# A hybrid decoder layer: the transposed projections of both token groups made once, during the first group's attention

## The chip, the core and the metric

The kernel runs on one core of a Trainium2 chip. The metric is the device time of one execution in microseconds (us), the median of several runs. Engines are named as in the profile: PE is TensorE (PEld its weight loads), DVE VectorE, ACT ScalarE, POOL GpSimd, SP SyncE, which here only issues DMAs.

## The reference, cut to what matters

1024 tokens of width 1024 go through one decoder layer. After an RMS norm, one weight gives seven projections: queries, keys, values and a gate for four retention heads, and queries, keys and values for four heads of differential attention. Then come the output projection with a residual, and a layer of 16384 single-neuron experts, of which each token takes 16 in each of 8 heads.

```python
h = rmsnorm(x, norm_mix_g); proj = h @ w_in
rq, rk, rv, rg, dq, dk, dv = jnp.split(proj, IN_OFFSETS, axis=-1)
ret_out  = silu(rg) * rmsnorm(retention(rq, rk, rv))            # chunks of 128 tokens, a state S carried on
diff_out = rmsnorm(diff_attention(dq, dk, dv, lam), g) * 0.2     # causal: two softmaxes, p1 - lam * p2
x = x + concat([ret_out, diff_out]) @ w_out
# peer: q = xn @ wq; scores s against sub-keys; top 16 of each half; top 16 of their sums -> experts e, gates g
x = x + einsum('thk,thkd->td', g * gelu(einsum('thkd,td->thk', u[e], xn)), v[e])
out = rmsnorm(x, final_norm_g)
```

## The kernel before, in words

Tokens lie in eight tiles of 128. They form two groups: tiles 0 to 2 (384 tokens, "sparse") and tiles 3 to 7 (640 tokens, "dense"). Every matmul operand in float32 is split into a high and a low part (`hi`, `lo`), and a product is three matmuls: hi·hi, lo·hi and hi·lo. A weight block of 512 KB is loaded into `wraw`, ACT makes `whi` (L152), DVE makes `wlo` (L154); `chunk` does this.

`front` is the path of one group up to its expert routing and is a generator: at each `yield` the program may switch to another one. Its stages are: norm and transpose into `hx` (tiles `hh`, `hl`); `proj_n`, the projections that come out token-major (values `rv` and `dv`, later the gate `rg`; PSUM tile `psN`, 512 columns); for each head `ret_proj` and `att_proj`, the projections that come out transposed (queries and keys; PSUM tile `psT`, 384 columns in the first group, two halves of 320 in the second); for each head and tile `retention` and `attention`; then `rg`, the mix, the output projection and its norm; then routing, whose many top-k instructions are DVE's. The projections of head h+1 are woven among the tiles of head h. `attention` for a tile is a chain across engines: scores on PE (`psS`), row maximum on DVE (`Z`, L349), exponentials on ACT (`e`), their difference on DVE (L358 to L361, one L359 per tile), transposes (`psA`) and the product with the values (`pov`) on PE.

The first group's experts are gathered, 768 times 512 KB by POOL with indices (L860 and L867), each followed by one DVE instruction: L862 (`ug`, with a small read of its accumulator) or L869 (`sa`). Five buffers (`ug`) hold what is under way. The second group's experts are computed densely, all 128 blocks of 128 neurons, in the last stage, which is matmuls (`psH`, `kp`, `psV`); its partial sums in `psV` are added by DVE at L830.

What sets the order: the program is written as loops and weaves, and a scheduler fixes the order on each engine when the kernel is built. A gathered instruction of DVE is held by `gate` behind a marked DVE instruction; marks are taken at the yields of the second group's way up to its routing, 1.5 at each:

```python
run(gated(weave(until(gd, "routing"), sparse_routes(...), ROUTE, 1), PER[:2]))   # PER = (1.5, 1.5, 0.0)
```

So the number of yields there sets how many gathered instructions may stand early; those without a mark of their own wait for the last mark, which lies at the first block of the last stage. The whole order of the front part is these lines:

```python
run(until(gs, "normed")); front_consts(cst, cp, wp); run(until(gs, "mixed"))
run(weave(until(gs, "summed"), until(gd, "normed"), 15, 5))
run(weave(until(gd, "projected"), gs, 8, 19))
```

Of the kernel before, what the change touches and what calls it, by code (L numbers as in the profile page):

```python
# [13 lines left out]
F32 = mybir.dt.float32  # L14
# [84 lines left out]
def layer_kernel(ctx, tc, x, wt, wn, wo, wq, sk, ut, u, v, gmix, gffn, gfin, gsub, dlam, consts, alb, out):  # L99
# [6 lines left out]
    kd_d = tc.dram_tile([H, 2, P, T], F32, name="kd_d")  # L106
# [24 lines left out]

    def front(m, pp, cst, g0, nt, dense, late):
# [13 lines left out]

        def chunk(src, shape):

            raw = wp.tile(shape, F32, tag="raw", bufs=RAW, name="wraw")
            SY.dma_start(raw, src)  # L150
            hi = wp.tile(shape, F32R, tag="uh", bufs=2, name="whi")
            A.activation(hi, raw, AF.Copy)  # L152
            lo = wp.tile(shape, F32R, tag="ul", bufs=2, name="wlo")
            V.tensor_sub(lo, raw, hi.bitcast(F32))  # L154
            return hi, lo

        def mm(ps, a, b, start, stop):

            PE.matmul(ps, a[0], b[0], start=start, stop=False)
            PE.matmul(ps, a[0], b[1], start=False, stop=False)  # L160
            PE.matmul(ps, a[1], b[0], start=False, stop=stop)

        def at(ops, *ix):
            return [o[ix] for o in ops]
# [62 lines left out]
        hx = yield from split_t(normed, "h")  # L227

# [11 lines left out]
        yield from proj_n([wn[8 + c] for c in range(4)], hx, put_dv)  # L240
        yield "projected"
# [11 lines left out]
        def ret_proj(h):  # L253
            qT = wp.tile([P, n], F32, tag="ga", bufs=2, name="qT")
            for a, b, ps in proj_t(wt[2 * h], hx):
                A.activation(qT[:, a:b], ps, AF.Copy)
            yield
            kT = ap.tile([P, n], F32, tag="kT", bufs=2, name="kT")
            for a, b, ps in proj_t(wt[2 * h + 1], hx):
                A.activation(kT[:, a:b], ps, AF.Copy, scale=P ** -0.5)  # L260
            ops[h] = [qT, kT]
            yield
# [30 lines left out]
        def att_proj(h):  # L293
            qa = [ap.tile([P, n], F32R, tag=f"q2{m}", bufs=2, name=f"qa{m}") for m in range(2)]
            qb = [ap.tile([P, n], F32R, tag=f"qb{m}", bufs=1, name=f"qb{m}") for m in range(2)]
            for a, b, ps in proj_t(wt[8 + 2 * h], hx):
                pt = ap.tile([P, b - a], F32, tag="pt", name="pt")
                A.activation(pt, ps, AF.Copy, scale=0.125)
                for m in range(2):
                    own, oth = slice(64 * m, 64 * m + 64), slice(64 - 64 * m, 128 - 64 * m)  # L300
                    A.activation(qa[m][own, a:b], pt[own], AF.Copy)
                    A.activation(qa[m][oth, a:b], pt[own], AF.Copy)
                    V.tensor_sub(qb[m][own, a:b], pt[own], qa[m][own, a:b].bitcast(F32))
                    V.tensor_sub(qb[m][oth, a:b], pt[own], qa[m][own, a:b].bitcast(F32))
            yield
            kk2 = ap.tile([P, 2, L], F32R, tag="kd", name="kk") if h % 2 else fp.tile([P, 2, L], F32R, tag="R", name="kk")
            kk = [kk2[:, m] for m in range(2)]
            if not first:
                for m, tl in enumerate(kk):
                    G.dma_start(tl[:, :lo0], kd_d[h, m][:, :lo0])  # L310
            for a, b, ps in proj_t(wt[8 + 2 * h + 1], hx):
                sl = slice(lo0 + a, lo0 + b)
                pt = ap.tile([P, b - a], F32, tag="pt", name="pt")
                A.activation(pt, ps, AF.Copy)
# [594 lines left out]
```

## Time and profile before

| | |
|---|---|
| median of 3 runs | 2905.25 us (2904.76 to 2907.47) |
| profiled execution, its own time | 2900.81 us |
| its span, first to last instruction | 2899.0 us |
| PE busy | 2712.1 us (94%) |
| DVE busy | 2363.5 us (82%) |
| ACT / POOL busy | 1063.9 us (37%) / 1047.4 us (36%) |
| granted PE clock, mean | 0.975 |

Busy time is the union of an engine's instructions; matmuls overlap in the pipeline, so a busy PE need not be working at its full rate. Read the table by stage rather than as a whole: the stages have different limits.

### The profile page before, as it was taken

The numbers are of one execution on the slowest core, as the hardware profiler recorded it, in microseconds if no ns is written. First come the engines' busy times: TensorE is split into PE (matmuls) and PEld (weight loads), VectorE is DVE, ScalarE is ACT, GpSimd is POOL, SyncE is SP. The second block draws the span as 40 slices with busy tenths as digits, with TensorE's granted clock in tenths as the row PEclk, the third lists the DMA queues.
The fourth block names the chain that finished last, engine by engine and source line by source line (L and its number), as shares of the span: only waits on it lengthen the run. The fifth ranks groups of instructions, "written<-read, shape, count | busy, mean of one in ns | idle before, by whom it ended". The sixth has DMA issues, their size and how long they took to land.

```text
span 2899.0 us, 43071 instructions
## 1 busy us (share of the span) xinstructions
PE 2712.1 (94%) x16043; PEld 2441.4 (84%) x16043; DVE 2363.5 (82%) x4547; ACT 1063.9 (37%) x1881; POOL 1047.4 (36%) x782
## 2 busy tenths in 40 slices
PE   7979988988889999998898998999999999999998
PEld 6868877876789999997787887899999999989987
DVE  3555899888589988985788887888889888888988
ACT  4653334544232369992222222222223222222222
POOL 0000004434310000003454443666565556655664
PEclk9989998999989999999999999999999999999999
DMA  5334236756742246668988898999999999999997
GB/s 167 105 126 146 95 113 234 242 195 236 246 150 82 87 153 236 250 257 299 313 303 285 307 326 289 347 321 344 337 333 351 325 345 341 336 343 326 341 339 259
DMA packets 292805, 741.34 MB, mean 256 GB/s; under 512 B 23401, under 2 KB 117609, under 8 KB 292594
## 3 DMA queue, kind: packets, MB, share of 16 engines
q0 software_dynamic: 111744, 404.28, 39.1%
q1 hardware_dynamic: 180850, 334.31, 33.4%
q8 instruction: 126, 2.06, 0.3%
q14 instruction: 85, 0.70, 0.1%
HBM read 670.14 MB, written 68.35 MB: 255 GB/s over the span
## 4 chain that ended last, share of the span: by engine, by line
PE 46%; DVE 14%; DMA 10%; issue 9%; POOL 3%; ACT 3%; SPq 0%; POOLq 0%; DVEq 0%; ACTq 0%
PE psH L721 6%; PE psH L722 6%; PE psH L720 6%; DMA gt<-g_d 4%; PE psV L794 4%; PE psV L795 3%; PE psV L796 3%; DMA ug<-in_u,idx 2%; PE kp L795 2%; PE kp L796 2%; PE kp L794 2%; PE psHs L720 2%; PE psHs L722 2%; DVE sa L869 2%; PE psHs L721 2%
## 5 line engine op out<-in xcount | busy, mean ns | idle before, releaser
L867 POOL DMA_INDIRECT vg<-in_v,idx x384 | 530.1, 1381 | 915.2 <-DVE ug L862 517.0
L860 POOL DMA_INDIRECT ug<-in_u,idx x384 | 511.9, 1333 | 502.7 <-DVE ug L862 335.4
L869 DVE SCALAR_TENSOR_TENSOR sa<-vg,shs,sa 128x1024 f32<-128x1024 f32 x384 | 491.9, 1281 | 40.5 <-DMA vg<-in_v,idx 36.9
L862 DVE SCALAR_TENSOR_TENSOR ug<-ug,sx 128x1024 f32<-128x1024 f32 x384 | 460.6, 1219 | 72.9 <-DMA ug<-in_u,idx 72.2
L720 PE MATMUL psH<-nh,uh 128*128 128x320 f32 x1424 | 439.6, 309 | 0.7 <-ACT uh L706 0.7
L721 PE MATMUL psH<-nl,uh 128*128 128x320 f32 x1424 | 439.7, 309 | 0.0
L722 PE MATMUL psH<-nh,ul 128*128 128x320 f32 x1424 | 438.6, 309 | 0.8 <-DVE ul L708 0.8
L794 PE MATMUL psV<-vh,wh 128*128 128x512 f32 x768 | 305.5, 399 | 29.3 <-DVE acc L830 27.5
L795 PE MATMUL psV<-vl,wh 128*128 128x512 f32 x768 | 304.4, 397 | 0.0
L796 PE MATMUL psV<-vh,wl 128*128 128x512 f32 x768 | 297.1, 397 | 0.0
L720 PEld LDWEIGHTS psH<-nh,uh 128*128 128x128 f32 x1424 | 267.4, 188 | 6.8 <-ACT uh L706 1.5
L721 PEld LDWEIGHTS psH<-nl,uh 128*128 128x128 f32 x1424 | 267.5, 188 | 5.1
L722 PEld LDWEIGHTS psH<-nh,ul 128*128 128x128 f32 x1424 | 267.2, 188 | 4.6 <-DVE ul L708 1.6
L723 ACT ACTIVATE ga<-psH 128x320 f32<-128x320 f32 x178 | 74.6, 426 | 407.5 <-PE psH L722 368.4
L706 ACT ACTIVATE uh<-uraw 128x1024 fp32r<-128x1024 f32 x128 | 135.6, 1059 | 207.1 <-PE psH L721 110.2
L720 PE MATMUL psHs<-nh,uh 128*128 128x320 f32 x624 | 197.0, 317 | 9.3 <-ACT ga L723 9.1
L154 DVE TENSOR_TENSOR wlo<-wraw,whi 128x1024 fp32r<-128x1024 f32 x104 | 126.7, 1219 | 93.0 <-ACT whi L152 90.9
L794 PEld LDWEIGHTS psV<-vh,wh 128*128 128x128 f32 x768 | 147.4, 192 | 61.9 <-DVE acc L830 30.5
L795 PE MATMUL kp<-vl,wh 128*128 128x512 f32 x512 | 198.3, 391 | 0.9 <-DVE vl L818 0.9
L152 ACT ACTIVATE whi<-wraw 128x1024 fp32r<-128x1024 f32 x104 | 110.0, 1058 | 241.6 <-PE psT L160 117.6
L794 PE MATMUL kp<-vh,wh 128*128 128x512 f32 x512 | 192.3, 391 | 5.3 <-ACT wh L810 5.3
L721 PE MATMUL psHs<-nl,uh 128*128 128x320 f32 x624 | 195.1, 313 | 0.0
(243 smaller groups left out, 6159.0 us busy)
## 6 DMA issues: line engine op xcount, KB each, us to landing
uraw<-in_ut SPq DMA_DIRECT2D x128, 512.0 KB, 6.3
vraw<-in_v SPq DMA_DIRECT2D x128, 512.0 KB, 6.8
g_d<-st SPq DMA_DIRECT2D x80, 512.0 KB, 4.9
gt<-g_d SPq DMA_DIRECT2D x32, 1280.0 KB, 18.0
wraw<-in_wt SPq DMA_DIRECT2D x32, 512.0 KB, 3.7
wraw<-in_wq SPq DMA_DIRECT2D x32, 512.0 KB, 3.7
hs_d<-ga SPq DMA_DIRECT2D x39, 320.0 KB, 2.5
gl<-hs_d SPq DMA_DIRECT2D x39, 320.0 KB, 6.8
```

Of the source, the lines that this page charges most:

```text
L154: V.tensor_sub(lo, raw, hi.bitcast(F32))
L706: A.activation(uh, raw, AF.Copy)
L720: PE.matmul(ps, uh[:, dc], xh[:, dc, sl], start=(dc == 0), stop=False)
L721: PE.matmul(ps, uh[:, dc], xl[:, dc, sl], start=False, stop=False)
L722: PE.matmul(ps, ul[:, dc], xh[:, dc, sl], start=False, stop=(dc == DC - 1))
L794: PE.matmul(ps, Wh[e][:, sl], Vh[e][:, so], start=start, stop=False)
L795: PE.matmul(ps, Wh[e][:, sl], Vl[e][:, so], start=False, stop=False)
L796: PE.matmul(ps, Wl[e][:, sl], Vh[e][:, so], start=False, stop=stop)
L860: G.indirect_dma_start(out=ug, out_offset=None, in_=u, in_offset=bass.IndirectOffsetOnAxis(ap=idxA[t][:, k:k + 1], axis=0))
L862: gate(V.scalar_tensor_tensor(ug, ug, 1.0, xt, op0=ALU.mult, op1=ALU.mult, accum_out=hs[:, k:k + 1]))
L867: G.indirect_dma_start(out=vg, out_offset=None, in_=v, in_offset=bass.IndirectOffsetOnAxis(ap=idxA[t][:, k:k + 1], axis=0))
L869: gate(V.scalar_tensor_tensor(ac, vg, hs[:, k:k + 1], ac, op0=ALU.mult, op1=ALU.add))
```

## The change

The projections of `ret_proj` and `att_proj` go into one generator, `heads`, which loads each of the 16 weight blocks once and multiplies it with the first group (384 columns) and with both halves of the second (2 x 320). It runs woven among the first group's attention. Of the first group, queries and keys of retention stay on chip; all else goes to DRAM (`qk_d`, `rq_d`) from where `loads` brings it back head by head, the attention operands in six DMAs of 64 partitions each, which replaces the partition copies by ACT and DVE in `att_proj`. In the second group `loads` fills two rooms that held `hx`. The second group's gate `rg` is projected with its values and goes through DRAM (`rg_d`). The second group's norm is woven into the first group's value projections.

On SP this takes off 16 weight loads and 8 stores of `kd_d`, and adds 16 stores to `rq_d`, 24 to `qk_d`, 5 to `rg_d`, 48 loads of 64 partitions from `qk_d`, 8 from `rq_d` and 1 from `rg_d`. On POOL it takes off the 8 loads of `kk`.

```diff
+    def heads(pp, xs, xd, ap, ops):
+        ns, hb = NS * P, TB // 2
+        for h in range(H):
+            ops[h] = []
+            for kind in range(4):
+                w = chunk(wt[2 * h + kind % 2 + (8 if kind > 1 else 0)], [P, DC, P])
+                ps1 = pp.tile([P, 512], F32, tag="T", name="psT")
+                two = pp.tile([P, 2, 512], F32, tag="A", bufs=2, name="psT2")
+                parts = [(xs, 0, ns, 0, ps1)] + [(xd, i * hb, hb, ns + i * hb, two[:, i]) for i in range(2)]
...
+                    for dc in range(DC):
+                        mm(ps, at(w, slice(None), dc), at(x_, slice(None), dc, slice(c0, c0 + n)),
+                           dc == 0, dc == DC - 1)
...
+                    A.activation(st[:, 0], ps, AF.Copy, scale=scale)
+                    V.scalar_tensor_tensor(st[:, 1], ps, scale, st[:, 0].bitcast(F32), op0=ALU.mult, op1=ALU.subtract)
+                    SY.dma_start(qk_d[h, kind - 2][:, :, t0:t0 + n].rearrange("s p t -> p s t"), st.bitcast(F32))
+                yield
...
+        def loads(h):
+            if not first:
+                r = [ap.tile([P, n], F32, tag=tg, bufs=2, name=tg) for tg in ("qT", "kT")]
...
+            for tl, rows, src in ((qa, lo, part(0, 0, lo0)), (kk, lo, part(1, 0, 0)), (kk, hi, part(1, 1, 0)),
+                                  (qa, hi, part(0, 0, lo0)), (qb, lo, part(0, 1, lo0)), (qb, hi, part(0, 1, lo0))):
+                SY.dma_start(tl.bitcast(F32)[rows], src)
...
-            nxt = chain(ret_proj(h + 1), att_proj(h + 1)) if h < H - 1 else iter(())
-            yield from weave(tiles, nxt, 2 * nt, 4)
+            nxt = ready(h + 1) if h < H - 1 else iter(())
+            yield from weave(tiles, nxt, 2 * nt, 5 if first else 1)
...
+        if dense:
+            SY.dma_start(rg, rg_d.rearrange("t p c -> p t c"))
...
+                run(weave(until(gs, "projected"), until(gd, "normed"), 8, 5))
                 run(until(gs, "mixed"))
-            run(weave(until(gs, "summed"), until(gd, "normed"), 15, 5))
-            run(weave(until(gd, "projected"), gs, 8, 19))
+            run(until(gs, "summed"))
+            run(weave(until(gd, "projected"), gs, 12, 19))
```

Rows of the built order follow; line numbers of the changed kernel differ from those before (L862 is now L905, L869 L912, L830 L873, L159 to L161 are L146 to L148, L341 to L346 are L371 to L376, L371 is L401).

On PE, in the second group's attention of a tile, before: behind the scores of one tile (`psS`) stand projections of the next head (`psT`), 24 of them to a half.

```order
L341 LDWEIGHTS ab
L341 MATMUL psS<-ab 128x256
L343 MATMUL psS<-kk,qa_4188 128x256
L344 MATMUL psS<-kk,qb_4190 128x256
L346 LDWEIGHTS identb
L346 MATMUL psS<-maskb,identb 128x128
L159 MATMUL psT<-hh,whi 128x320
L160 MATMUL psT<-hl,whi 128x320
L161 MATMUL psT<-hh,wlo 128x320
```

The same place in the changed kernel (`roomhTh`, `roomhTl` are the rooms with keys, queries and values):

```order
L371 LDWEIGHTS ab
L371 MATMUL psS<-ab 128x128
L373 MATMUL psS<-roomhTh,roomhTl 128x128
L374 MATMUL psS<-roomhTh,roomhTl 128x128
L376 LDWEIGHTS identb
L376 MATMUL psS<-maskb,identb 128x128
L401 MATMUL pov<-roomhTh,aT 128x128 x8
L330 MATMUL ret<-qT,kT 128x128
L337 MATMUL ret<-rv,am 128x128
L339 MATMUL ret<-S,qT 128x128
```

The projections are gone from between the tiles; scores are followed by the work of the tile before and by retention.

On PE, in the first group's attention of the changed kernel, the second group's projections (320 columns, `psT_1063`) stand among the tiles:

```order
L146 MATMUL psT_1063<-hh,whi 128x320
L401 MATMUL pov<-dvh,aT 128x128
L147 MATMUL psT_1063<-hl,whi 128x320
L148 MATMUL psT_1063<-hh,wlo 128x320
L146 MATMUL psT_1063<-hh,whi 128x320
L147 MATMUL psT_1063<-hl,whi 128x320
L148 MATMUL psT_1063<-hh,wlo 128x320
L334 MATMUL ret<-ident,kT 128x128
L146 MATMUL psT<-hh,whi 128x384
```

All 768 of them moved here, from 37 places ahead of the second group's attention and the rest inside it.

On DVE, the end of the program before: the last gathered row (`sa`) stands ahead of these, and after the last addition of a `psV` (`accab`) come final norms alone.

```order
L776 SCALAR_TENSOR_TENSOR fin<-fa,rs_f,gfb 128x1024
L776 SCALAR_TENSOR_TENSOR sfin<-sa,rs_f,gfb 128x1024
L830 TENSOR_TENSOR accab<-psV,accab 128x512
L839 COPY fa<-accc_intra 128x512
L129 RECIPROCAL rs_f<-rs_f 128x1
L839 COPY fa<-accab 128x512
L776 SCALAR_TENSOR_TENSOR fin<-fa,rs_f,gfb 128x1024
L129 RECIPROCAL rs_f<-rs_f 128x1
L776 SCALAR_TENSOR_TENSOR fin<-fa,rs_f,gfb 128x1024
```

The same place in the changed kernel; behind these rows stand only the norm of the gathered tile (`sfin`):

```order
L873 TENSOR_TENSOR accab<-psV,accab 128x512
L912 SCALAR_TENSOR_TENSOR sa<-vg,shs,sa 128x1024
L882 COPY fa<-accc_intra 128x512
L882 COPY fa<-accab 128x512
L131 RECIPROCAL rs_f<-rs_f 128x1
L912 SCALAR_TENSOR_TENSOR sa<-vg,shs,sa 128x1024
L819 SCALAR_TENSOR_TENSOR fin<-fa,rs_f,gfb 128x1024
L912 SCALAR_TENSOR_TENSOR sa<-vg,shs,sa 128x1024
L131 RECIPROCAL rs_f<-rs_f 128x1
L912 SCALAR_TENSOR_TENSOR sa<-vg,shs,sa 128x1024
L819 SCALAR_TENSOR_TENSOR fin<-fa,rs_f,gfb 128x1024
L912 SCALAR_TENSOR_TENSOR sa<-vg,shs,sa 128x1024 x18
```

Counted along DVE, 124 gathered instructions stand ahead of the last stage before and 100 in the changed kernel, and behind the last addition (`accab`) none before and 22 in the changed kernel. Between the second group's first routing product and the last stage the order is the same in both on PE and DVE.

## Rows read from the trace of the kernel before

**Rows 1.** The page: busy time, share of span and instructions of each engine.
```profile
PE 2712.1 (94%) x16043; PEld 2441.4 (84%) x16043; DVE 2363.5 (82%) x4547; ACT 1063.9 (37%) x1881; POOL 1047.4 (36%) x782
```
**Rows 2.** Windows by stage; columns as the first line names them.
```profile
core 0: us, PE busy (x) PEld busy (x) DVE busy (x) ACT busy (x) POOL busy (x), PEclk, DMA share, GB/s
0.00:58.00 58.00, 41.09 (x168) 32.59 (x169) 21.92 (x35) 24.71 (x35) 0.69 (x6) 1.00 0.52 161
58.00:199.00 141.00, 124.76 (x735) 111.62 (x734) 67.72 (x136) 83.92 (x223) 0.00 (x0) 0.97 0.36 119
199.00:407.00 208.00, 188.11 (x983) 165.45 (x984) 152.07 (x706) 72.37 (x120) 0.00 (x0) 0.96 0.37 125
407.00:457.00 50.00, 42.35 (x269) 39.49 (x269) 49.30 (x118) 18.97 (x38) 4.46 (x6) 0.97 0.33 101
457.00:701.00 244.00, 204.86 (x1269) 177.71 (x1269) 204.21 (x378) 116.79 (x308) 117.20 (x98) 0.92 0.70 234
701.00:825.00 124.00, 102.61 (x473) 84.70 (x472) 87.40 (x166) 40.98 (x73) 40.01 (x31) 0.89 0.68 240
825.00:1304.00 479.00, 465.47 (x3906) 452.02 (x3905) 430.46 (x1414) 303.57 (x519) 1.87 (x2) 1.00 0.47 171
1304.00:2890.00 1586.00, 1542.86 (x8253) 1377.78 (x8251) 1345.99 (x1593) 400.24 (x563) 883.12 (x639) 0.99 0.92 324
```
**Rows 3.** Timeline of PE: start, us, instruction; back-to-back matmuls of 320 and 512 columns.
```profile
429.73 0.31 PE L159 MATMUL psT<-hh,whi 128*128 128x320 f32 x1
429.88 0.31 PE L160 MATMUL psT<-hl,whi 128*128 128x320 f32 x1
...
168.27 0.39 PE L159 MATMUL psN<-whi,hh 128*128 128x512 f32 x1
168.50 0.39 PE L160 MATMUL psN<-wlo,hh 128*128 128x512 f32 x1
```
**Rows 4.** Group by line, whole span: count | busy us, mean ns | idle before, releasers.
```profile
L159 PE MATMUL psT<-hh,whi 128*128 128x384 f32 x128 | 44.6, 348 | 6.1 <-ACT pt L298 2.2 <-ACT kT L260 1.3 <-ACT qT L256 1.2
```
**Rows 5.** DMAs by line: count, KB each, us to landing.
```profile
kd_d<-kk SPq DMA_DIRECT2D x8, 192.0 KB, 3.2
kk<-kd_d POOLq DMA_DIRECT2D x8, 192.0 KB, 4.6
```
**Rows 6.** Windows of two stages, matmuls on tile psT alone.
```profile
199.00:407.00 208.00, 75.93 (x421) 0.96 0.37 125
457.00:701.00 244.00, 89.09 (x504) 0.92 0.70 234
```
**Rows 7.** Groups of DVE by line in 457 to 701 us.
```profile
L862 DVE SCALAR_TENSOR_TENSOR ug<-ug,sx 128x1024 f32<-128x1024 f32 x92 | 110.5, 1219 | 24.5 <-DMA ug<-in_u,idx 24.2
L154 DVE TENSOR_TENSOR wlo<-wraw,whi 128x1024 fp32r<-128x1024 f32 x11 | 13.4, 1218 | 3.3 <-ACT whi L152 3.3
...
L862 DVE DVE_READ_ACCUMULATOR ug<-ug,sx 128x1 f32 x92 | 7.5, 81 | 0.0
L318 DVE TENSOR_TENSOR kk<-pt,kk 64x320 fp32r<-64x320 f32 x12 | 5.8, 486 | 0.4
...
L359 DVE TENSOR_SCALAR rz<-rz,Z,nlam 128x1 f32<-128x1 f32 x19 | 5.1, 270 | 0.3
```
**Rows 8.** Windows of 10 us in which PE had little to do.
```profile
200.00:210.00 10.00, 3.75 (x14) 2.65 (x14) 8.85 (x28) 4.22 (x8) 0.00 (x0) 0.50 0.38 128
800.00:810.00 10.00, 3.07 (x14) 2.70 (x15) 9.57 (x17) 2.60 (x7) 5.11 (x4) 0.54 0.93 337
```
**Rows 9.** Group of PE by line in 701 to 790 us.
```profile
L159 PE MATMUL psN<-whi,hh 128*128 128x512 f32 x25 | 9.3, 393 | 0.0
```
**Rows 10.** Timeline of POOL, first and last of 11 gathers near the end.
```profile
2856.20 1.86 POOL L867 DMA_INDIRECT vg<-in_v,idx  x1 [0.66 <-DVE sa L869]
...
2873.35 0.94 POOL L867 DMA_INDIRECT vg<-in_v,idx  x1 [0.30 <-issue]
```
**Rows 11.** Timeline of DVE: the last addition and the last instruction.
```profile
2890.43 0.68 DVE L830 TENSOR_TENSOR accab<-psV,accab 128x512 f32<-128x512 f32 x1
...
2893.78 1.28 DVE L776 SCALAR_TENSOR_TENSOR fin<-fa,rs_f,gfb 128x1024 f32<-128x1024 f32 x1
```

More of the change, by code (lines that the diff above doesn't have):

```diff
@@ L130, in rstd, with chunk, mm @@
         return r
+    def chunk(src, shape):
+        raw = wp.tile(shape, F32, tag="raw", bufs=RAW, name="wraw")
+        SY.dma_start(raw, src)
+        hi = wp.tile(shape, F32R, tag="uh", bufs=2, name="whi")
+        A.activation(hi, raw, AF.Copy)
+        lo = wp.tile(shape, F32R, tag="ul", bufs=2, name="wlo")
+        V.tensor_sub(lo, raw, hi.bitcast(F32))
+        return hi, lo
+    def mm(ps, a, b, start, stop):
+        PE.matmul(ps, a[0], b[0], start=start, stop=False)
+        PE.matmul(ps, a[0], b[1], start=False, stop=False)
+        PE.matmul(ps, a[1], b[0], start=False, stop=stop)
@@ L145, in big @@
             return m.big[0].tile(shape, dt, tag=m.big[1], bufs=m.big[2], name=name)
[L147 to L164, printed above, removed]
         def proj_t(src, xs, tags="TT"):
@@ L227, in front @@
         hx = yield from split_t(normed, "h")
+        m.own["hx"] = hx
         yield "normed"
@@ L240, in front, with put_rg @@
         yield from proj_n([wn[8 + c] for c in range(4)], hx, put_dv)
+        def put_rg(t, ps):
+            g = big([P, 512], "rgt")
+            A.activation(g, ps, AF.Silu)
+            SY.dma_start(rg_d[t], g)
+        if dense:
+            yield from proj_n([wn[4 + c] for c in range(4)], hx, put_rg)
         yield "projected"
@@ L291, in retention @@
                 yield
[L293 to L314, printed above, removed]
-                for m in range(2):
-                    own, oth = slice(64 * m, 64 * m + 64), slice(64 - 64 * m, 128 - 64 * m)
-                    A.activation(kk[m][own, sl], pt[own], AF.Copy)
-                    V.tensor_sub(kk[m][oth, sl], pt[own], kk[m][own, sl].bitcast(F32))
-            if not last:
-                for m, tl in enumerate(kk):
-                    SY.dma_start(kd_d[h, m][:, lo0:L], tl[:, lo0:].bitcast(F32))
-            ops[h] += [qa, qb, kk]
-            yield
@@ L375, in attention, with ready @@
                 yield
-        yield from ret_proj(0)
-        yield from att_proj(0)
+        def ready(h):
+            if first:
+                yield from islice(projs, 4)
+            yield from loads(h)
+        rooms = [] if first else [m.hp.tile([P, DC * n], F32R, tag=tg, name="room" + tg) for tg in ("hTh", "hTl")]
+        projs = heads(pp, hx, m.other["hx"], ap, ops) if first else None
+        yield from ready(0)
         for h in range(H):
             tiles = weave(retention(h), attention(h))
-            nxt = chain(ret_proj(h + 1), att_proj(h + 1)) if h < H - 1 else iter(())
-            yield from weave(tiles, nxt, 2 * nt, 4)
+            nxt = ready(h + 1) if h < H - 1 else iter(())
+            yield from weave(tiles, nxt, 2 * nt, 5 if first else 1)
         yield "mixed"
         rg = fp.tile([P, nt, 512], F32, tag="R", name="rg")
-        yield from proj_n([wn[4 + c] for c in range(4)], hx,
-                          lambda t, ps: A.activation(rg[:, t], ps, AF.Silu))
+        if dense:
+            SY.dma_start(rg, rg_d.rearrange("t p c -> p t c"))
+        else:
+            yield from proj_n([wn[4 + c] for c in range(4)], hx,
+                              lambda t, ps: A.activation(rg[:, t], ps, AF.Silu))
         rr = rstd(fp, msr, P, "r")
@@ L742, in layer_kernel @@
             ms.big = md.big = (sp, *ug)
+            ms.own = md.other = {}
+            md.own = ms.other = {}
             lates = Routed(sp, sn, ("sx", "sa"))
```

58 lines of the change are left out of this document (44 added, 14 removed).

## Prediction

> **What bounds the kernel now.** I read the page first: PE is busy for 94% of the span and DVE for 82% [rows 1], which says that two engines are near full, but not where. So I cut the span into stages, at the times where the first and last instructions of each stage stand, and read busy time per stage [rows 2]. The reader should see four different regimes. From 0 to 199 us (the first group's norm, projections and attention) PE is busy for 166 of 199 us and DVE for 90: PE and the latency of the chain are the limit, DVE has room. From 199 to 407 us (mix of the first group, its routing, the second group's value projections) PE is still the fuller one, 188 of 208 us. From 407 to 457 us the routing is decoded and DVE is full, 49.3 of 50 us. From 457 to 701 us (the second group's attention, woven with its projections and the first gathers) DVE and PE are both at 84%, 204 and 205 of 244 us. Behind 825 us order and work stay the same up to 1304 us; the last stage is dense matmuls, PE 1543 of 1586 us, with DVE at 85% because 644 of the 768 gathered instructions run there.
>
> **What the change removes, adds and moves.** The number of projection matmuls is the same; the change moves 16 x 2 x 24 = 768 of them, 320 columns each, from the second group's attention into the first group's. What it really removes is on DVE and ACT: 16 weight splits and the partition copies. I cost it stage by stage.
>
> *0 to 199 us.* Back to back, a matmul of 320 columns follows the one before at 0.147 us (0.15 between the two starts shown) [rows 3]: 768 x 0.147 = 113 us of PE. (The second group's 31 remaining transposes move from the next stage to this one; a few us that cancel in the sum, left out of both.) What can absorb them is PE's idle time. In 58 to 199 us it is 141.0 - 124.8 = 16 us [rows 2], and of this 6 us are waits for ACT to empty `psT` [rows 4]; they go, because now two other PSUM tiles lie between two uses of the same one. I take 113 - 6 = +107 us. Below: all 16 us are filled, +97. Above: the way through DRAM shows once, at the last head, where nothing stands behind it. The nearest rows are the old store and load of keys, 3.2 and 4.6 us [rows 5]: 113 + 8 = +121. Elsewhere the next head's projections (four weights) cover these transfers, and weight loads queued behind a waiting store on SP have four buffers; a weight lasts PE 48 x 0.147 = 7 us in the second group's columns alone.
>
> *199 to 407 us.* The second group's gate comes here: 4 x 5 x 2 x 3 = 120 matmuls of 512 columns at 0.23 us [rows 3], 28 us. Out go 421 - 384 = 37 projections (the 384 are routing's) [rows 6], 5 us. That is +23 if nothing is filled; PE idles for 20 us here [rows 2], and 120 matmuls that wait for nobody should fill half of it: +13, between +3 and +23.
>
> *407 to 457 us.* DVE is the limit. It loses five splits and twelve subtractions that stand here (by their durations in rows 7: 6.1 and 5.8 us) and gets four more attention tiles (five instead of one by the order): 49.3 - 11.9 + 4 x 2.92 (next paragraph) = 49.1. So 0.
>
> *457 to 701 us.* DVE's 204.2 us are 92 gathered instructions, 110.5 + 7.5 = 118.0 us or 1.283 each; 11 splits, 13.4 us; three groups of 12 subtractions like the one shown, 17.4 us; and the rest, 55.4 us, is the attention of 19 tiles (19 times L359), 2.92 us each [rows 7]. In the changed order 71 gathers and 15 tiles stand here: 71 x 1.283 + 15 x 2.92 = 134.9 us. Now how long does this take? If DVE keeps its 84%, 161 us. If a tile keeps its 244 / 19 = 12.84 us, 15 of them take 193 us: then the chain of scores, maximum, exponentials and transposes sets the pace, not DVE's sum. Both can be defended, so I take the middle, 177 us: -67. Below: DVE as full as in the stage before, 134.9 / 0.986 = 137 us, -107. Above: nothing is saved, 244 us, because PE now waits in each tile where it used to project. DMA should not be the limit: 71 x 0.52 MB + about 11 MB of operands in 177 us is 270 GB/s, against 324 GB/s that the last stage holds for 1586 us [rows 2].
>
> *701 to 825 us.* The gate is no longer projected here: 25 x 3 matmuls [rows 9] x 0.23 = 17 us. -17, between -8 (part of it hid the wait for the mix) and -21 (three gathers fewer on DVE as well).
>
> *From 1304 us.* Only 100 gathered instructions stand ahead of this stage, not 124, because the second group's way has fewer yields and so fewer marks. The stage's matmuls are PE's, so it lasts as long as before, and the order gives it about the same number of gathers, 646 against 644; the other 22 stand behind the last addition. This is the cost that a list of removed instructions does not show. Eleven gathers near the end were issued 17.15 us apart from first to last, 1.715 us each, with no wait but POOL's own [rows 10]. 22 x 1.715 = 38 us, less 2 us as five buffers are full at the start: +36. What follows the last gather (a norm and one store) is what follows the last addition before, 2890.4 us against a span of 2899.0 us [rows 11]. Below: DVE's pace of 1.283 us, +28. Above: the slowest issue of those rows, 1.86 + 0.30 us, +47.
>
> **The sum.** 107 + 13 + 0 - 67 - 17 + 36 = +72 us. The profiled execution took 2900.8 us, the median of the runs 2905.25 us; the differences apply to both, and I add to the median: 2905 + 72 = **2977 us**. All low ends: 97 + 3 - 107 - 21 + 28 = 0 us. All high ends: 121 + 23 + 0 - 8 + 47 = +183 us.
>
> **A rule weighed against the trace.** Where PE had little to do, its granted clock fell to half, 1.2 of 2.4 GHz: 0.50 at 200 to 210 us, with PE busy for 3.75 of 10 us, and 0.54 at 800 to 810 us, with 3.07 of 10 [rows 8]. In 457 to 701 us, with projections in every gap, it was 0.92 [rows 2]. The Trainium skill, "TensorE: Matmul & The Clock Gate", section "HAM oscillation — how this bites in real kernels", says that an array left idle between bursts is throttled again, so that each burst starts cold. By that rule the change takes away what kept the clock up, and the attention would run cold; these rows agree with it. What it would cost is the first rival.
>
> **The rivals.** *First: the attention runs at half clock.* PE's work there without the projections is 204.9 - 89.1 = 116 us [rows 2, 6] for 19 tiles, 6.1 each, in which a clock of 0.92 is already contained; at half clock 15 tiles take about 15 x 6.1 x 0.84 = 77 us more. If half of that lies beside DVE's work, the stage takes 177 + 38 = 215 us, and the kernel 2977 + 38 = 3015 us; if all of it is on the path, 3054 us. For it: the two low windows. Against it: they had PE at a third, here it would be near half.
>
> *Second: no tail.* The 22 gathers run beside matmuls, because DVE comes to them sooner than the built order lets one think: +36 falls away, 2941 us. Against it: DVE takes its instructions in order, and the last addition waits for PE's last matmul.
>
> *Third, the other side: DVE's work is what sets the time of the front part.* Then moved matmuls cost nothing and only DVE's sum counts: 16 splits of 1.218 us, 20 us; the old subtractions less the new ones, some 25 us; 24 gathers, 31 us; with the tail of 36 us the kernel would take 2905 - 76 + 36 = 2865 us. For it: DVE full in 407 to 457 us and at 84% behind it. Against it: up to 199 us DVE works for 90 us, and this is where the matmuls land. It decides once the first two stages grow by less than 120 - 72 = 48 us together.
>
> That the change does not do what it says is not among them: the order shows one load per weight and the moved matmuls.
>
> **How the numbers follow.** My forecast, a sum between +40 and +105 us, gets 0.60; the first rival 0.17; the second 0.10; the third 0.08; the rest, 0.05, is the forecast with nearly all low ends, between no change and +40. The range leaves out the third rival, the far end of the first and a part of the rest: 2925 to 3045 us; the likeliest case alone is 2945 to 3010 us. Less than 0.2% (6 us) is about what a measurement of this kernel cannot tell from no change: faster 0.08, same 0.02, slower 0.90.
>
> **What would show it.** Right: PE near full and DVE half idle up to about 310 us; the first gather near 577 us instead of 457; about 177 us from there to the second mix, with DVE busier than PE; the stage of 479 us as before; and at the end some 36 us in which only POOL and DVE work. Wrong: the first stage much shorter than 300 us, since then the chain and not PE's sum held it; or a second attention that takes 215 us and more at a clock near 0.5; or gathers that end with the matmuls.

## The result and the profile after

The changed kernel takes 3011.24 us (median of 4 runs, 3005.96 to 3017.3) against 2905.69 us for the kernel before (median of 4): a ratio of 1.0363, 95% interval 1.034 to 1.0387. That is 105.5 us more, where +72 was forecast, with a range from +20 to +140. The profiled execution is the longest of the four, 3017.3 us; by the profiles alone the difference is 116 us of span.

The page of the changed kernel, busy time by engine; it answers to [rows 1]:
```profile
PE 2735.2 (91%) x16043; PEld 2457.7 (82%) x16043; DVE 2322.3 (77%) x4483; ACT 1015.5 (34%) x1792; POOL 1082.1 (36%) x774
```
The number of PE's instructions is the same; DVE does 41 us less work, and the kernel is longer all the same. So again by stage. Windows of the changed kernel, columns as in [rows 2]:
```profile
0.00:58.00 58.00, 41.43 (x186) 33.61 (x187) 32.12 (x52) 33.67 (x56) 0.70 (x6) 1.00 0.65 214
58.00:302.00 244.00, 234.28 (x1516) 226.33 (x1514) 66.78 (x134) 85.30 (x227) 0.00 (x0) 0.99 0.40 121
302.00:532.00 230.00, 209.91 (x1047) 181.48 (x1047) 147.52 (x691) 73.64 (x112) 0.00 (x0) 0.96 0.44 133
532.00:594.00 62.00, 40.45 (x197) 29.88 (x197) 52.44 (x137) 20.00 (x56) 5.03 (x5) 0.75 0.60 177
594.00:771.00 177.00, 109.31 (x572) 83.17 (x572) 134.42 (x257) 65.78 (x200) 88.56 (x69) 0.77 0.73 232
...
2970.00:3015.00 45.00, 0.00 (x0) 0.00 (x0) 32.22 (x30) 3.66 (x9) 23.88 (x17) 0.53 0.75 258
```
The reader sees the forecast's picture: from 58 to 302 us PE full and DVE about a quarter busy; a second attention of 177 us in which DVE is busier than PE; 45 us at the end in which PE does nothing. New is that PE is no longer near its limit anywhere between 532 and 771 us, and that DVE is not full in the decode either (52.44 of 62 us).

To compare many kernels I cut each trace at instructions of DVE, not at round times. Cut *a* is where DVE comes to the first product of the first mix (retention's output times its gate), *b* the start of the decode (the sum of the gates), *c* the end of the last copy of decoded indices, *d* the first product of the second mix, *e* the first product of the last stage (activations times gates), *f* the end of the last addition into an accumulator. Lengths between the cuts in the profiled execution of each kernel, in us (the kernels from the third row on are the experiments):

| kernel | 0–a | a–b | b–c | c–d | d–e | e–f | f–end | median of runs |
|---|---|---|---|---|---|---|---|---|
| before | 198.2 | 213.8 | 48.8 | 256.8 | 612.2 | 1561.2 | 7.9 | 2905.69 |
| changed | 302.1 | 234.6 | 43.9 | 190.5 | 612.4 | 1586.2 | 45.4 | 3011.24 |
| e1_marks | 303.0 | 234.4 | 43.8 | 203.8 | 619.7 | 1561.2 | 8.2 | 2979.63 |
| e2_fewer | 197.9 | 213.5 | 48.7 | 255.3 | 605.1 | 1580.1 | 45.6 | 2951.02 |
| e3_gate | 199.1 | 235.1 | 50.9 | 249.8 | 606.5 | 1565.4 | 8.5 | 2919.69 |
| e4_two | 266.6 | 234.9 | 43.9 | 183.3 | 612.4 | 1580.7 | 44.6 | 2968.73 |
| e5_fill | 305.6 | 234.6 | 45.1 | 203.0 | 609.5 | 1584.8 | 44.6 | 3029.57 |
| e6_sx | 305.2 | 234.1 | 43.9 | 181.9 | 613.4 | 1578.4 | 44.7 | 3005.23 |
| e7_once | 303.3 | 234.8 | 53.5 | 166.9 | 615.1 | 1567.9 | 44.6 | 2988.95 |
| e8_more | 198.8 | 214.2 | 48.8 | 270.5 | 615.6 | 1553.8 | 8.5 | 2913.25 |
| e9_none | 303.7 | 235.2 | 44.0 | 130.5 | 595.1 | 1578.3 | 202.1 | 3090.77 (1 run) |
| e10_none_b | 199.1 | 213.9 | 46.4 | 211.6 | 598.7 | 1579.0 | 199.6 | 3050.31 (1 run) |
| e11_both | 304.8 | 234.8 | 43.9 | 198.3 | 619.1 | 1571.0 | 8.4 | 2980.99 |
| e12_cover | 197.9 | 211.8 | 51.9 | 262.3 | 613.1 | 1563.9 | 7.9 | 2910.45 |

The first two rows give the difference by its parts: +103.9, +20.8, -71.2 (b to d), +0.2, +25.0, +37.5: 116.2 us. Forecast were +107, +13, -84 (0 - 67 - 17), 0, 0, +36 (the 17 us are the gate, whose matmuls lay almost wholly ahead of *d*). Three terms are off: the stage that got the gate, the stretch from b to d, and the last stage, which was to keep its length and did not.

Two of these losses can be read in the changed kernel's trace. In the first, DVE stands at its first gathered product, as the waits of DVE in 532 to 594 us say (us in total, times, longest):
```profile
DVE ug L905 <- DMA sx<-xn_d: 7.7, 1, 7.7
```
`sx`, the input row of the gathered experts, is loaded by SP. Timeline of SP in the changed kernel; its loads stand in a row:
```profile
571.59 0.58 SPq L319 DMA_DIRECT2D roomhTl<-qk_d  x1
572.26 1.23 SPq L319 DMA_DIRECT2D roomhTh<-qk_d  x2
573.54 1.90 SPq L319 DMA_DIRECT2D roomhTl<-qk_d  x3
575.54 0.54 SPq L897 DMA_DIRECT2D sx<-xn_d  x1
591.27 0.38 SPq L358 DMA_DIRECT2D roomhTh<-dv_d  x1
```
Six loads of a head's operands were issued just ahead of `sx`, and the first gathered product starts only at 593.8 us, 18 us after the load was issued. In the kernel before the same load took 3.7 us from issue to landing (DMAs of 400 to 470 us; KB, us):
```profile
sx<-xn_d SPq DMA_DIRECT2D x1, 512.0 KB, 3.7
```
In the changed kernel the DMA engines had no free time in these 18 us, as the window from the issue to the landing says (columns as in [rows 2]; the DMA share is the last number but one, and 1.04 means all the time):
```profile
575.50:593.80 18.30, 13.51 (x76) 10.14 (x76) 8.79 (x19) 7.18 (x19) 2.90 (x3) 0.81 1.04 281
```
This wait is the price of the way through DRAM, in a place where the forecast had not looked: the operands were in time, but together with the first gathers (POOL issues five of them at 571 to 583 us) they held the DMA engines while `sx` was due. The second loss is at the start of the last stage. Windows of its first 100 us and of the whole stage, first of the kernel before, then of the changed one:
```profile
1329.90:1429.90 100.00, 88.19 (x420) 73.85 (x419) 80.69 (x88) 20.93 (x29) 49.80 (x35) 0.98 0.87 302
1329.90:2891.10 1561.20, 1519.32 (x8098) 1355.04 (x8096) 1338.99 (x1589) 387.64 (x546) 883.12 (x639) 0.99 0.92 324
```
```profile
1383.50:1483.50 100.00, 81.14 (x360) 66.16 (x359) 72.57 (x104) 14.82 (x21) 49.22 (x36) 0.91 0.82 286
1383.50:2969.70 1586.20, 1527.64 (x8097) 1360.08 (x8095) 1338.28 (x1612) 385.74 (x541) 915.93 (x646) 0.98 0.91 320
```
In the first 100 us PE gets 60 matmuls fewer done, at a granted clock of 0.91 instead of 0.98, while DVE runs 16 instructions more. Over the whole stage PE idles 16.7 us longer and is busy 8.3 us longer with as many matmuls.

### The profile page after: what moved, and what is told of

It reads as the page before. It is cut to its first block, busy times and chain, and to the rows that moved or that the text cites. A ratio compares the mean times of both kernels' runs of the same rounds, so it can differ in the third digit from the quotient of the medians.

```text
span 3015.1 us, 43047 instructions
## 1 busy us (share of the span) xinstructions
PE 2735.2 (91%) x16043; PEld 2457.7 (82%) x16043; DVE 2322.3 (77%) x4483; ACT 1015.5 (34%) x1792; POOL 1082.1 (36%) x774
## 4 chain that ended last, share of the span: by engine, by line
PE 46%; issue 25%; DMA 13%; DVE 10%; POOL 5%; ACT 1%; SPq 0%; POOLq 0%; DVEq 0%; ACTq 0%
DMA gt<-g_d 5%; PE psH L761 4%; PE psH L762 4%; PE psH L760 4%; POOL vg L910 3%; PE psV L837 3%; PE psV L838 3%; PE psV L839 3%; PE psT L146 3%; PE psT L147 3%; PE psT L148 3%; DMA ug<-in_u,idx 2%; PE psN L146 2%; PE psN L147 2%; PE psN L148 2%
## 5 line engine op out<-in xcount | busy, mean ns | idle before, releaser
L903 POOL DMA_INDIRECT ug<-in_u,idx x384 | 542.1, 1412 | 1494.7 <-DVE ug L905 817.9
L910 POOL DMA_INDIRECT vg<-in_v,idx x384 | 539.4, 1405 | 425.0 <-DVE sa L912 330.8
L905 DVE SCALAR_TENSOR_TENSOR ug<-ug,sx 128x1024 f32<-128x1024 f32 x384 | 460.4, 1221 | 89.1 <-DMA ug<-in_u,idx 80.8
L912 DVE SCALAR_TENSOR_TENSOR sa<-vg,shs,sa 128x1024 f32<-128x1024 f32 x384 | 492.2, 1282 | 42.8 <-DMA vg<-in_v,idx 38.2
L141 DVE TENSOR_TENSOR wlo<-wraw,whi 128x1024 fp32r<-128x1024 f32 x88 | 108.1, 1229 | 143.3 <-ACT whi L139 133.7
L762 PE MATMUL psHs<-nh,ul 128*128 128x320 f32 x624 | 193.2, 314 | 0.8 <-DVE ul L748 0.8
```

The costliest lines, as they stand in the source:

```text
L762: PE.matmul(ps, ul[:, dc], xh[:, dc, sl], start=False, stop=(dc == DC - 1))
L903: G.indirect_dma_start(out=ug, out_offset=None, in_=u, in_offset=bass.IndirectOffsetOnAxis(ap=idxA[t][:, k:k + 1], axis=0))
L905: gate(V.scalar_tensor_tensor(ug, ug, 1.0, xt, op0=ALU.mult, op1=ALU.mult, accum_out=hs[:, k:k + 1]))
L910: G.indirect_dma_start(out=vg, out_offset=None, in_=v, in_offset=bass.IndirectOffsetOnAxis(ap=idxA[t][:, k:k + 1], axis=0))
L912: gate(V.scalar_tensor_tensor(ac, vg, hs[:, k:k + 1], ac, op0=ALU.mult, op1=ALU.add))
```

## The experiments

Ratios are to the kernel before as it ran beside each experiment, at 2905.6 to 2906.9 us. The order on each engine is fixed anew for every kernel that is built, so an edit also shifts instructions that it does not name. Its size can be read from e4: it leaves the work from *b* to *d* as it is in the changed kernel, and in its own order this stretch is 7.2 us shorter. A difference of that size between two single profiles in there shows nothing by itself.

**The marks (e1, e2, e8).** A gathered product is held back in the built order by a mark; yields of the front part set the marks. e1 gives the changed kernel its marks back, e2 takes as many from the kernel before.
```diff
-PER = (1.5, 1.5, 0.0)
+PER = (1.9, 1.9, 0.0)
```
The same line reads `(1.2, 1.2, 0.0)` in e2 and `(1.8, 1.8, 0.0)` in e8.

> The changed kernel with 1.9 instead of 1.5 marks per yield: 127 gathered instructions stand ahead of the last stage instead of 100 (18 of the 27 in the second group's attention), and none behind its last addition instead of 22. Theory A: the missing marks made both the tail of 36 us and the 25 us by which the last stage grew, since 28 instead of 4 instructions of the first gathered tile and its Gelu now stand at that stage's start; DVE has 43 us of room in the second attention, so I give the 18 instructions there (23 us of DVE) half of their time, +10 us: 3011 - 36 - 25 + 10 = 2960 us, last stage back to 1535 us. Theory B: the 25 us have another cause that came with the moved projections; only the tail goes: 3011 - 36 + 10 = 2985 us, last stage 1560 us.

Measured: 2979.63 us, ratio to before 1.025 (1.0228 to 1.0272), 31.6 us less than the changed kernel. The last stage is back at 1561.2 us and the tail at 8.2 us; from b to e the 27 instructions cost 20.5 us, 0.76 each. (The expectations of e1 and e2 count the last stage from a later point: their 1535 and 1560 us are some 1561 and 1586 us between *e* and *f*.) Tail and stage side with theory A. The time itself lies nearer B's 2985 than A's 2960 us, since the gathers that came forward cost twice what was put for them, and since the 25 us are the upper end of that loss, as e2 shows next.

> The kernel before with 1.2 instead of 1.5 marks per yield: 99 gathered instructions ahead of the last stage instead of 124, 22 behind its last addition instead of none; no projection moves. Theory A (fewer marks cost the tail and the growth of the last stage): +36 + 25, less what 20 fewer instructions give back in the second attention (26 us of DVE, of which half, 13 us): 2906 + 48 = 2954 us, last stage 1560 us. Theory B (only the tail): 2906 + 36 - 13 = 2929 us, last stage 1535 us.

Measured: 2951.02 us, ratio 1.0156 (1.0131 to 1.0181), +44 us, with no projection moved: theory A. Windows of e2, the last stage and what follows its last addition:
```profile
1320.50:2900.60 1580.10, 1522.55 (x8098) 1355.87 (x8096) 1341.46 (x1615) 384.44 (x540) 891.87 (x647) 0.99 0.92 322
2900.60:2946.10 45.50, 0.00 (x0) 0.00 (x0) 32.64 (x30) 4.33 (x9) 23.54 (x17) 0.52 0.73 256
```
The reader sees the changed kernel's end, with PE at nothing in the last 45 us, in a kernel whose attention is that of before. So theory A holds in both directions: the missing marks make the tail and lengthen the last stage. The six kernels with 124 or more instructions ahead of that stage have it at 1554 to 1571 us, mean 1563; the eight with 100 or fewer at 1568 to 1586, mean 1579. The two kinds meet at their edges (e7 and e11), and the loss is about 17 us in the mean; the 25 of the profile after are the upper end. That kernels without any gathered instruction ahead of it (e9, e10) have 1579 us as well says that it does not grow with their number; what goes with it is the built order at the stage's start, which has 31 to 33 of them among the first eight experts in the kernels of the second kind, against 25 to 28 in the first. That this order is the cause was not tested by itself.

> The kernel before with 1.8 instead of 1.5 marks per yield: 149 gathered instructions ahead of the last stage instead of 124; the other runs showed that 25 fewer cost 44 us. Theory A: the gain ends with the tail, which is gone already at 124; the 25 more cost 0.4 us each in the front part and give back little: 2907 + 10 - 5 = 2912 us. Theory B: the last stage goes on shrinking by 0.8 us for each instruction that is out of it: 2907 + 10 - 20 = 2897 us.

Measured: 2913.25 us, ratio 1.0025 (1.0009 to 1.0041). From b to e +17 us for 25 more gathers, behind e 7 us less. Theory A: more marks than before had give nothing.

**The gate alone (e3).** In the kernel before, the part of the change's diff that has `put_rg`, `rg_d`, the `if dense` at `rg` and the last weave at 12 to 19 steps, and no other part of it; the marks stand at 1.6 per yield (both not shown here).
```diff
+        if dense:
+            yield from proj_n([wn[4 + c] for c in range(4)], hx, put_rg)
...
+            SY.dma_start(rg, rg_d.rearrange("t p c -> p t c"))
```


> The kernel before with one part of the change alone: the second group's gate is projected behind its value projections and goes through DRAM (marks set to 1.6 per yield, so that 126 gathered instructions stand ahead of the last stage). Theory A: the gate's matmuls add their whole 28 us to the stage of mix and routing, and take 17 us out of the second mix: 2906 + 28 - 17 = 2917 us. Theory B, the prediction's term: they fill half of the idle 20 us, +18 - 17: 2907 us; the rest of what that stage grew by in the changed kernel came with the moved projections.

Measured: 2919.69 us, ratio 1.0047 (1.003 to 1.0063), +12.8 us. The stage from a to b grows by 21.3 us, as in the changed kernel (20.8). Window of e3 from a to b:
```profile
199.10:434.20 235.10, 218.86 (x1129) 191.84 (x1128) 162.31 (x736) 84.52 (x134) 2.35 (x4) 0.97 0.39 126
```
Of the 26.7 us that PE works more than before (192.2 between the same cuts), 21.3 lengthen the stage: a fifth was filled, not half. From b to e 10.6 us come back. Theory A is nearer, and this edit by itself makes the kernel slower.

**What sets the first attention (e4).** The second group's projections without the product with the weight's low part.
```diff
-                        mm(ps, at(w, slice(None), dc), at(x_, slice(None), dc, slice(c0, c0 + n)),
-                           dc == 0, dc == DC - 1)
+                        a, b = at(w, slice(None), dc), at(x_, slice(None), dc, slice(c0, c0 + n))
+                        if t0 == 0:
+                            mm(ps, a, b, dc == 0, dc == DC - 1)
+                        else:
+                            PE.matmul(ps, a[0], b[0], start=dc == 0, stop=False)
+                            PE.matmul(ps, a[0], b[1], start=False, stop=dc == DC - 1)
```


> The changed kernel with the third of the three matmuls left out of the second group's transposed projections (256 of 768 matmuls of 320 columns, the product with the weight's low part; the rest is as it was). Theory A: PE's sum sets the first group's attention: 256 x 0.147 us = 38 us less, the stage 302 - 38 = 264 us, the kernel 2973 us. Theory B: the chain of scores, ACT's emptying of PSUM and the way through DRAM set it: at most half of that, the stage 283 us or longer, the kernel 2992 us or more.

Measured: 2968.73 us; up to a 266.6 instead of 302.1 us. 256 matmuls fewer give 35.5 us, 0.139 each, where 0.147 was expected: theory A, PE's sum.

**The way through DRAM (e6, e7, e11).** e6 loads `sx` from POOL's queue; e7 loads the second group's attention operands for the first head only and uses them for all four; e11 is e1 and e6 together. First the edit of e6, then that of e7:
```diff
-        SY.dma_start(xt, xn_d[t])
+        G.dma_start(xt, xn_d[t])
```
```diff
+            if not first and h:
+                ops[h] += ops[0][2:]
+                yield
+                return
...
-            SY.dma_start(dvh, dv_d[:g0 + nt, :, h * P:(h + 1) * P].rearrange("t p c -> p t c"))
+            if first or h == 0:
+                SY.dma_start(dvh, dv_d[:g0 + nt, :, h * P:(h + 1) * P].rearrange("t p c -> p t c"))
```


> The changed kernel with the load of the gathered experts' input rows (sx) issued from POOL's queue instead of SP's, so that it does not stand behind the loads of the heads' operands. Theory A: the 13 us by which the decode stage grew are DVE standing at its first gathered instruction for this load (7.7 us) and what queues behind it: first gather at about 583 instead of 593.8 us, the kernel 8 to 13 us shorter, 3000 us. Theory B: DVE has room in the attention that follows and catches up, so the wait only moves: 3011 us, and the second mix at 771 us as it is.

Measured: 3005.23 us, ratio to before 1.0342 (1.0319 to 1.0365): 6 us less than the changed kernel, with intervals that overlap. From b to d it is 8.6 us shorter, little more than what e4 has there without touching `sx`. POOL issues the load at 577.88 us, and the timeline of DVE in e6 shows what still comes of it:
```profile
591.16 1.22 DVE L905 SCALAR_TENSOR_TENSOR ug<-ug,sx 128x1024 f32<-128x1024 f32 x1 [2.27 <-DMA sx<-xn_d]
```
13 us from issue to landing instead of 18: the queue of another engine does not help much against the six transfers that are under way.

> The changed kernel with the second group's attention operands (q, k and v of the differential heads) loaded for the first head only and used for all four; about 8.6 MB of reads and their waits on SP's queue are left out. Theory A: the way through DRAM holds the second attention (DMA share 0.73, waits for dvh and in SP's queue): the stage shrinks from 177 to about 160 us or less, and the kernel by 15 us or more, 2996 us. Theory B: the loads are hidden but for the 2.9 us wait that the trace shows: 3008 us.

Measured: 2988.95 us, ratio 1.0287 (1.0259 to 1.0314), 22 us less. Theory A has the size and not the place: the stretch from the first gathered product to d stays at 177.1 us (177.3 in the changed kernel); what goes is the wait ahead of it, since DVE comes to the first gathered product 43.3 us after b, as in the kernel before (43.8), and no longer 57.1. `sx` lands 3.9 us after its issue (DMAs of 560 to 595 us):
```profile
sx<-xn_d SPq DMA_DIRECT2D x1, 512.0 KB, 3.9
```
Window of e7 for these 43.3 us:
```profile
538.10:581.40 43.30, 31.61 (x132) 22.91 (x132) 42.55 (x101) 16.12 (x47) 4.84 (x2) 0.70 0.21 73
```
DVE is full again and the DMA share 0.21. Of the 13.8 us, 8.8 are idle time of DVE that is gone (the wait for `sx` above all); the other 5 are decode work that stands behind the first gather in e7's order. The rest of the gain lies in a last stage of 1567.9 us, the shortest with 100 instructions ahead of it; why, stays open.

> The changed kernel with both mends: 1.9 marks per yield, and sx loaded from POOL's queue. Theory A: they add up, 2980 - 6 = 2974 us, and what is left over the kernel before is the first attention's +103, the gate's +22 and 13 back, less the second attention's 71. Theory B: with 18 more gathered instructions in the second attention the earlier start is worth more, since DVE is the fuller engine there: 2965 us or less.

Measured: 2980.99 us, ratio 1.0249 (1.0217 to 1.0281): no better than e1, and over what either theory gave. The second attention is 5.5 us shorter from c to d, the last stage 10 us longer. So the gain from `sx` on POOL is not shown by any time of a whole kernel.

**The clock in the second attention (e5).** Matmuls that nobody reads, behind the scores of each tile.
```diff
+                if not first:
+                    fill = pp.tile([P, 512], F32, tag="T", name="fill")
+                    for f in range(12):
+                        PE.matmul(fill, identb, cst["albr"][:, :512], start=f == 0, stop=f == 11)
```


> The changed kernel with 12 matmuls that nobody reads (128x512, bf16, into the PSUM bank that is free there) behind the scores of each of the 20 tiles of the second group's attention; an estimate by the 0.23 us that 512 columns take is 240 x 0.23 = 55 us more for PE, which idles for 68 of the 177 us there. Theory A: the chain of scores, DVE and gathers sets that stage, and the granted clock of 0.77 costs nothing on the path: the clock rises and the stage stays within 177 to 187 us, the kernel at 3011 to 3021 us. Theory B: the low clock costs time; at the clock of 0.92 that the stage had before, PE's own 109 us become 91 us, and the stage shrinks by up to 18 us: 2993 us.

Measured: 3029.57 us, 18 us more than the changed kernel and over the upper end of theory A. Windows of e5, b to c and c to d:
```profile
540.20:585.30 45.10, 42.48 (x233) 25.28 (x234) 43.85 (x104) 11.80 (x34) 3.08 (x3) 1.00 0.39 118
585.30:788.30 203.00, 134.35 (x724) 96.42 (x728) 137.84 (x265) 72.93 (x219) 87.38 (x74) 0.84 0.70 223
```
From b to c the clock is at its upper level throughout (0.73 in the changed kernel) and the stretch 1 us longer; from c to d it rises from 0.78 to 0.84, and the stretch is 12.5 us longer. So from b to c the low clock was not what the stretch waited for. From c to d the run can't say it: PE is busy 15 us longer with the added matmuls, and whether a high clock that costs nothing would shorten the stretch stays open.

**The second attention without gathers (e9, e10).** No marks at all, in the changed kernel and in the one before; one run each.
```diff
-PER = (1.5, 1.5, 0.0)
+PER = (0.0, 0.0, 0.0)
```


> The changed kernel with no marks at all: no gathered instruction stands ahead of the last stage, and 114 instead of 22 behind its last addition, so the whole is far slower; only the second group's attention, from the end of the decode to the second mix (177 us), is asked for. Theory A: that stage has the gathers on its path nearly one for one; 18 more of them cost 14 us, so 72 fewer give back about 55 us: some 122 us. Theory B: the chain of scores, maximum, exponentials and transposes sets it and the gathers lie in its gaps: 160 us or more.

> The same for the kernel before: no marks, no gathered instruction ahead of the last stage; only the stretch from the end of the decode to the second mix (262 us, of which PE works for 222) is asked for. Theory A: PE's sum sets it there, and the gathers lie beside: 235 to 255 us. Theory B: the gathers are on the path as in the changed kernel, 0.4 to 0.8 us each: 262 - 40 = 222 us or less, which PE's own work hardly allows.

Measured, windows from c to d: the changed kernel, e9, the kernel before, e10.
```profile
580.50:771.10 190.60, 119.37 (x637) 91.06 (x635) 138.56 (x266) 69.33 (x211) 91.15 (x72) 0.78 0.75 237
```
```profile
583.00:713.50 130.50, 103.99 (x638) 78.31 (x636) 58.38 (x122) 67.21 (x209) 2.42 (x3) 0.93 0.28 74
```
```profile
460.80:717.70 256.90, 217.76 (x1328) 188.12 (x1327) 214.19 (x400) 121.64 (x315) 121.17 (x101) 0.92 0.71 240
```
```profile
459.40:671.00 211.60, 199.87 (x1333) 175.15 (x1332) 109.90 (x213) 121.51 (x317) 4.95 (x7) 0.99 0.17 55
```
This is the table that the forecast lacked. Without projections 72 gathered instructions cost 60 us, 0.83 each (with the wait for `sx` in it; the 18 more of e1 cost 0.74 each). With projections beside them, 94 cost 45 us, 0.48 each. That is a mean and no fixed price: in the kernel before, 20 gathers fewer in this stretch (e2) save 1.5 us, and 19 more (e8) cost 13.7 us, 0.72 each, near the price without projections. So the cover may have been about used up; single profiles in orders of their own don't show it. And look at the clock: the same 637 or 638 matmuls of the changed kernel take PE 119.4 us with gathers and 104.0 without, at 0.78 and 0.93. What lies between, the waits show. DVE's group of gathered products in 594 to 771 us of the changed kernel, which answers to the first of [rows 7]:
```profile
L905 DVE SCALAR_TENSOR_TENSOR ug<-ug,sx 128x1024 f32<-128x1024 f32 x71 | 85.2, 1222 | 34.0 <-DMA ug<-in_u,idx 26.2 <-DMA sx<-xn_d 7.7
```
Waits of PE and of ACT in the same window, and then those of e9 from c to d (us in total, times, longest):
```profile
PE ret L330 <- ACT rv L349: 26.1, 11, 7.1
PE psA L397 <- DVE e L390: 20.4, 6, 12.2
...
ACT jk L347 <- DVE S L343: 38.8, 9, 9.0
```
```profile
PE ret L330 <- ACT rv L349: 4.7, 10, 0.8
...
PE psA L397 <- DVE e L390: 2.4, 5, 0.7
...
ACT jk L347 <- DVE S L343: 18.6, 7, 4.8
```
DVE takes its instructions in order; where it stands at a gather that hasn't landed or works through some, the tile's weights `e` behind them come late, and so does retention's state `S`, on which ACT stands before it empties `ret`. PE waits for both, and the clock falls. Loads of operands are not the difference: PE's wait for `dv_d` is 2.9 us with gathers and 3.1 without, and e7 keeps its 177.1 us with most of the loads left out. The low clock is a consequence; what part of the 60 us it adds in its turn, no run separates. (The 177 and 262 us of the expectations count from the first gathered product; from c on it is 190.5 and 256.8.) e9 sides with A, by 60 us for 72 gathers where 55 were expected. e10 sides with B: the gathers are on the path in the kernel before too, only for half the price, and without them PE fills 94% of the stage.

**The other way round (e12).** If projections are the cover, more of them should go under the attention: in the kernel before, each group's gate is projected transposed beside the last head's tiles, which had no projections. The diff is cut to that; the gate's product with retention's output moves behind the transposes.
```diff
+        def gate_proj():
+            for h in range(H):
+                for a, b, ps in proj_t(wt[16 + h], hx):
+                    A.activation(gT[:, h, a:b], ps, AF.Copy)
+                yield
...
-            nxt = chain(ret_proj(h + 1), att_proj(h + 1)) if h < H - 1 else iter(())
+            nxt = chain(ret_proj(h + 1), att_proj(h + 1)) if h < H - 1 else gate_proj()
```


> The kernel before, changed the other way round: the gate of each group is projected transposed, head by head, woven into the last head's attention (which had no projections beside it), its Silu and the product with the retention's output come behind the transposes (16 DVE operations of 128x512 more), and the mix starts without it. Theory A: projections are the cover under which attention, DVE and gathers run, so the last heads' gaps take them: PE idles for 13.6 of the 61 us of 640 to 701 us and for 12.5 of the 25 us of 185 to 210 us; the gate's 45 us leave the two mixes and return only by what these gaps cannot take; less half of the gaps, 13 us: 2906 - 13 = 2893 us. Theory B: the chain of the last head is what it was, the gate's matmuls only delay its scores, and DVE has 16 x 0.68 = 11 us more: 2906 to 2917 us.

Measured: 2910.45 us, ratio 1.0017 (1.0003 to 1.0031). No gain: theory B. From b to d it is 8.6 us longer, and the second gate's matmuls stand in this stretch in both kernels (106 of 120 in the one before). No version tried beats the kernel before; of the changed ones that do the whole work the best is e1.

## Why the forecast was right, and where it was off

**The sign and its reason: right.** What is saved is DVE's and ACT's work; what is paid is PE's, in a stage where PE was the limit. Up to a, +107 was forecast and +103.9 measured, and e4 shows the mechanism. The waits for `psT`, counted as 6 us to be saved, are gone: a group of PE by line and shape in the changed kernel, against 6.1 us idle in [rows 4]:
```profile
L146 PE MATMUL psT<-hh,whi 128*128 128x384 f32 x128 | 44.0, 344 | 0.0
```
**The gate: mis-sized.** "120 matmuls that wait for nobody should fill half of it: +13"; it was +20.8, and e3 has 21.3 with the gate and its weave alone. The idle time of an engine is not free room. PE's idle time from a to b went from 21.6 to 16.2 us in e3 and no further. In the kernel before, the waits of PE that sum highest in 199 to 407 us are short ones for ACT (us in total, times, longest):
```profile
PE psc L445 <- ACT pqT L437: 7.6, 6, 1.3
PE psN L159 <- ACT whi L152: 5.1, 6, 1.0
```
The term took half of such time as free.

**407 to 457 us: a wait was missed.** "So 0" was right for DVE's sum, 47.6 us busy from b to the first gathered product against the 49.1 worked out, but the stretch became 57.1 us long. The step that failed is the one that costs the way through DRAM: it asked whether the operands come in time, and the ends given were for their own latency. What came late was `sx`, behind them: 7.7 us of DVE's wait, which e7 takes away with the loads.

**The second attention: 177 us forecast and measured, by luck.** The number was the middle between DVE at 84% (161) and a constant pace per tile (193). Neither is a law: from c to d the stretch takes 190 us with gathers and 130 without, and the gathers add what the work beside them does not cover. The middle hit because their exposed part happened to lie between.

**The last stage: a term was missing.** "The stage's matmuls are PE's, so it lasts as long as before" failed: +25 in the profile, about 17 over all kernels. The count of 22 instructions behind the last addition was right, and so was their price: +37.5 against +36. POOL issues them one after the other, as in [rows 10]; timeline of POOL in the changed kernel, two of them:
```profile
2985.32 1.73 POOL L910 DMA_INDIRECT vg<-in_v,idx  x1 [0.30 <-issue]
2987.35 1.63 POOL L910 DMA_INDIRECT vg<-in_v,idx  x1 [0.30 <-issue]
```
But the row of gathers also begins 24 instructions further back, and the start of the stage, where DVE's queue holds additions that PE waits for, gets more of them. PE's waits for these additions, by line over the whole span, before and after:
```profile
L794 PE MATMUL psV<-vh,wh 128*128 128x512 f32 x768 | 305.5, 399 | 29.3 <-DVE acc L830 27.5
```
```profile
L837 PE MATMUL psV<-vh,wh 128*128 128x512 f32 x768 | 308.5, 403 | 41.7 <-DVE acc L873 34.9 <-DVE room L873 6.1 <-DVE accc_intra L873 0.6
```
That is 12 of the 25 us; the rest was not followed up.

**The rivals.** *Half clock*: the clock fell as feared, though to 0.77 and not to half, and the stage had the forecast's length anyway; e9 shows the clock as an effect of waits. The Trainium skill, "TensorE: Matmul & The Clock Gate", section "HAM oscillation — how this bites in real kernels", has PE throttled again when it idles between bursts; the granted clocks of 0.78 with and 0.93 without gathers agree. *No tail*: false, until the marks are given back (e1). *DVE's sum sets the front part*: false, up to b the kernel grew by 125 us, where it decided at 48.

## What to carry to other kernels

Idle DVE or PE time beside a full engine is cover, and work that waits for transfers lives on it, up to a point: before moving the covering work elsewhere, price the covered work without it (here 0.74 to 0.83 us per gathered instruction instead of 0.48 in the mean). When a schedule is paced by counts of program steps, a change that removes steps moves other work too: count it on both sides, and look where it lands and not only what is left at the end. For a new way through DRAM ask who else's load stands behind it.

## What the runs showed of the hardware

A load of 512 KB that took 3.7 us took 18 us behind six others, with the DMA engines busy throughout, and still 13 us from another engine's queue. The same 638 matmuls took PE 119 us with gathers beside them and 104 without, at granted clocks of 0.78 and 0.93. And the last stage, with DVE's instructions in the same order, took from 1580.7 to 1586.2 us in the profiled executions of three kernels (changed, e4, e5): a single profile doesn't resolve less than these 5.5 us there.
